# SSD mixer: channel tiles in pairs, one f32 run for a pair's mixed parts and the next pair's turns, states with 256 moving columns

## The chip, the cores and the metric

The kernel runs on one core of a Trainium2 chip. The metric is the device time of one execution in microseconds, median of several. A profile is one execution recorded by the hardware profiler. The engines are PE (matrix multiply, with PEld its weight loads), DVE (vector), ACT (activation functions, copies, casts), POOL (hardly used here) and SP (issues the DMAs). Each works through its own queue in order and waits at semaphores for the others.

## The reference

A trunk of two layers over 512 tokens and 1024 channels. Layer 0 mixes with Mamba-2 SSD, layer 1 with HGRN2; each has a squared-ReLU MLP, post-LayerNorm and a gated embedding. The change concerns the SSD mixer alone: 2048 inner channels (32 heads of 64), 4 groups, state size 128, chunks of 128 tokens.

```python
z, xbc, dt = jnp.split(u @ w_in, [SSD_D_INNER, SSD_D_INNER + SSD_CONV_DIM], axis=-1)
xbc = jax.nn.silu(causal_depthwise_conv(xbc, conv_w, conv_b))
xs, bm, cm = jnp.split(xbc, [SSD_D_INNER, SSD_D_INNER + SSD_BC_DIM], axis=-1)
...
cb = jnp.einsum('bclgn,bcsgn->bcgls', cm, bm)
y_diag = jnp.einsum('bcgls,bcgrls,bcsgrp->bclgrp', cb, decay, xdt)
decay_to_end = jnp.exp(a_cs[:, :, -1:] - a_cs)
states = jnp.einsum('bclgn,bclgr,bclgrp->bcgrpn', bm, decay_to_end, xdt)
...
y_off = jnp.einsum('bclgn,bcgrpn,bclgr->bclgrp', cm, prev, jnp.exp(a_cs))
y = y_diag + y_off + d_skip.astype(jnp.float32).reshape(g_, r_)[:, :, None] * xs
y = y.reshape(bsz, seq, SSD_D_INNER) * jax.nn.silu(z.astype(jnp.float32))
y = rms_norm(y.reshape(bsz, seq, g_, SSD_D_INNER // g_), norm_w.reshape(g_, SSD_D_INNER // g_))
return y.reshape(bsz, seq, SSD_D_INNER).astype(u.dtype) @ w_out
```

## The kernel before

The SSD inner channels form 16 tiles of 128 channels (two heads each), indexed j; four tiles are one group, with one B and one C projection per group. The loop `for j in range(17)` (L740 on) runs over them. For a tile:

- `x_part(j)` and `z_part(j)`: two projections. `project` splits weights into a high and a low f32r part (ACT casts `whi`, L110; DVE subtracts `wlo`, L112) and issues 24 f32r matmuls of 512 moving columns (L116 to L118). Weights are loaded from HBM by SP (L103) into 3 raw buffers and split into 6 pairs of buffers ahead of their use. x goes through a convolution of four taps (one step on ACT, L570, three on DVE, L573) and SiLU (L574) to `xs`; z through SiLU to `sz`.
- `turn_x(j)`: four PE transposes of xs (L635), read by DVE into `xw` (L639) and `xdt` (L641).
- `decays(j)`: from a table of cumulative decays (`csd`, loaded by DMA into `a`) DVE and ACT make `m` (L654, L659, L660), `ecs` (L658, L661) and `cd`.
- `states(j)`: three f32 matmuls of 128 moving columns (L669) and five short DVE operations that form `pv` (L675 to L678).
- `mixed(j)`: 14 f32 matmuls of half width, two beside each other in the array's column halves (L687, L689).
- `finish(j)`: DVE forms y (L705, L706), ACT and DVE its f32r parts `ys` (L708, L709), ACT squares it (L711) and DVE adds the square to `ss` of the group (L715).

`rms_group(g)` sums `ss` over channels by matmuls (L721) and makes `ri`; `pieces(g)` then gives the eight parts of the group's output projection (L250 adds them to `acc`), issued two at a time between the tiles. `bc_prep` makes `btok` and `cbm` for a group (L598, L604, L600, L606). The last group's output projection is `out_project`, with layer norm, transposes and their split (L230, L235, L236) chunk by chunk, behind which the MLP starts.

PE's order is that of the program text (`manual_schedule`); the orders of DVE, ACT and SP are set by a scheduler that goes by priorities, and are fixed when the program is built. PSUM has eight banks: four for projections (`psj`), and one each for `pt`, `pm`, `py0`, `py1`. In the loop a step for j runs: x projection, `states(j - 1)`, `mixed(j - 2)` and `finish`, z projection, `turn_x(j)`, `decays(j)`, two pieces. The f32 work of a tile so stands in two runs on PE: states with mixed, and the turn.

Of the kernel before, what the change touches and what calls it, by code (L numbers as in the profile page):

```python
# [15 lines left out]
P = 128  # L16
T = 512
NCH = 4
# [23 lines left out]
def trunk(ctx: ExitStack, tc, a):  # L42
# [27 lines left out]

    two = dict(cv=2, cm=2, cbm=2, pv=2)
    mlp = dict(r=8, blk=2, sg=2)
    bufs = dict(ssd=dict(two, xs=3, sz=3, btok=2, xdt=2, xw=2, ecs=2, ss=2), mlp0=mlp, hgrn=dict(qx=2, f=2, k=4, qo=2, qt=4, xc=2, gg=2, tot=4, sc=2, scd=2, btok=2), mlp1=mlp)
    phase = []
# [14 lines left out]
    def bank(p, tag):  # L89
        return mk(p, [P, T], tag)  # L90
# [445 lines left out]
    nc.vector.scalar_tensor_tensor(r1, up, -1.0, ab, ALU.add, ALU.subtract)  # L536
    ru = row("cbm")
    nc.vector.reciprocal(ru, up)
# [55 lines left out]

    def bc_prep(bcm, pt, spare):
# [5 lines left out]
        pc = bank(psy, spare)  # L601
# [10 lines left out]
    prep, live, decay = {}, {}, {}  # L612

# [6 lines left out]
    def z_part(j):  # L620
        ps = projected(10 * (j // 4) + 3 + 2 * (j % 4))
        sz = tmp("sz", [P, T])
        nc.scalar.activation(sz, ps, AF.Silu)
        live[j].append(sz)

# [4 lines left out]

    def turn_x(j, pt):
        dt_tok, w_tok, cs_tok = toks
        xs = live[j][0]
        for c in range(NCH):
            nc.tensor.transpose(pt[:, c * P : (c + 1) * P], xs[:, c * P : (c + 1) * P], ident)  # L635
        hs = slice(2 * j, 2 * j + 2)
        ptv = pt.rearrange("p (c h q) -> p c h q", c=NCH, h=2)
        xw = tmp("xw", [P, 3, 2, 64])
        nc.vector.tensor_mul(xw, ptv[:, 0:3], bc(w_tok[:, 0:3, hs], 3, 64))  # L639
        xdt = tmp("xdt", [P, NCH, 2, 64])  # L640
        nc.vector.tensor_mul(xdt, ptv, bc(dt_tok[:, :, hs], 3, 64))  # L641
        live[j] += [xw, xdt]

    def decays(j):
        dt_tok, w_tok, cs_tok = toks
        csb = decay.pop(j)
        btok, cbm, cm = prep[j // 4]
        cd = mk(sm, [P, 2, NCH], "cd")
        nc.scalar.activation(cd, csb.rearrange("p h (c l) -> p h c l", c=NCH)[:, :, :, P - 1], AF.Exp)
        m = mk(w4, [P, 2, T], "b")  # L650
# [10 lines left out]
        nc.vector.tensor_mul(ecs, ecs, bc(cm[:, P:], 1, 2))  # L661
        live[j] += [cd, m, ecs]

    def states(j):
        xs, sz, xw, xdt, cd, m, ecs = live[j]
        btok = prep[j // 4][0]
        pst_ = bank(psm, "pm")
        for c in range(3):
            nc.tensor.matmul(  # L669
                pst_[:, c * P : (c + 1) * P], btok[:, c, :], xw[:, c].rearrange("p h q -> p (h q)"), start=True, stop=True  # L670
            )
        pv = tmp("pv", [P, 3, 2, 64])
        stv = pst_[:, : 3 * P].rearrange("p (c h q) -> p c h q", c=3, h=2)
        with tc.high_priority(offset=LEAD + SOON):
            nc.vector.tensor_copy(pv[:, 0], stv[:, 0])  # L675
            for c in range(1, 3):
                nc.vector.tensor_mul(pv[:, c], pv[:, c - 1], bc(cd[:, :, c], 2, 64))
                nc.vector.tensor_add(pv[:, c], stv[:, c], pv[:, c])  # L678
        live[j].append(pv)

    def mixed(j):
        xs, sz, xw, xdt, cd, m, ecs, pv = live.pop(j)
        yd = bank(psy, "py%d" % (j % 2))
# [33 lines left out]
    def rms_group(g, pr):  # L717

        for c in range(NCH):
            for r in range(0, P, 64):  # L720
                nc.tensor.matmul(  # L721
                    pr[r : r + 64, 64 * c : 64 * c + 64], ss[g][:, c * P + r : c * P + r + 64], ones_s, start=True, stop=True
                )
# [13 lines left out]
    outs = iter(())  # L737
    bcm = {}
    with tc.manual_schedule(engines={mybir.EngineType.PE}):
        for j in range(17):  # L740
            if j < 16:
                load_decay(j)
                if j % 4 == 0:
                    bcm[j // 4] = bc_group(j // 4)
                x_part(j)
            if j == 0:
                z_part(0)
                continue
            if j == 4:
# [3 lines left out]
            if j == 1:  # L753
                z_part(1)
                prep[0] = bc_prep(bcm[0], bank(pst, "pt"), "py0")
                toks.extend(dt_tail())
                turn_x(0, bank(psy, "py1"))
                decays(0)
                continue
            if j == 2:  # L760
                turn_x(1, bank(pst, "pt"))
                decays(1)
                states(0)
                z_part(2)
                states(1)
                finish(0, *mixed(0))
                turn_x(2, bank(pst, "pt"))
                decays(2)
                continue
            if j == 16:  # L770
                next(outs), next(outs)
            states(j - 1)
            done = mixed(j - 2)
            if j % 4 == 2 and j > 2:
                outs = pieces(j // 4 - 1, rms_group(j // 4 - 1, bank(psy, "py1")))
            finish(j - 2, *done)
            if j < 16:
                z_part(j)
                if j % 4 == 0:
                    prep[j // 4] = bc_prep(bcm[j // 4], bank(psm, "pm"), "py1")  # L780
                turn_x(j, bank(pst, "pt"))
                decays(j)
                next(outs, None), next(outs, None)
        next(outs)
        finish(15, *mixed(15))
        next(outs)
        for _ in outs:
            pass
    h_s, *after = norm(0)
# [493 lines left out]
```

## Time and profile before

| | |
|---|---|
| median of 3 runs | 1422.53 us (1421.46 to 1422.73) |
| profiled execution | 1422.3 us, span 1420.5 us |
| granted clock of PE | 1.00 |
| SSD loop in the trace | from about 15 to 350 us |
| DVE in 350 to 390 us (output projection of the last group, norm) | 38.85 us busy |

In the profile a line number is that of the source line that issued an instruction; a helper's line (L110, L116) collects all its callers, so the names of the tiles tell which work it is. A row of a group gives busy time, mean duration of one in ns, and the idle time of the engine before it with what ended it. In a timeline each row gives start, length, engine, line, and in brackets the wait ahead. PE's matmuls are pipelined: a row's length is longer than the distance to the next, and the distance is what a matmul costs.

### The profile page before, as it was taken

The numbers are of one execution on the slowest core, as the hardware profiler recorded it, in microseconds if no ns is written. First come the engines' busy times: TensorE is split into PE (matmuls) and PEld (weight loads), VectorE is DVE, ScalarE is ACT, GpSimd is POOL, SyncE is SP. The second block draws the span as 40 slices with busy tenths as digits, with TensorE's granted clock in tenths as the row PEclk, the third lists the DMA queues.
The fourth block names the chain that finished last, engine by engine and source line by source line (L and its number), as shares of the span: only waits on it lengthen the run. The fifth ranks groups of instructions, "written<-read, shape, count | busy, mean of one in ns | idle before, by whom it ended". The sixth has DMA issues, their size and how long they took to land.

```text
span 1420.5 us, 20454 instructions
## 1 busy us (share of the span) xinstructions
PE 1413.6 (100%) x8143; PEld 1182.3 (83%) x8143; DVE 1025.4 (72%) x1713; ACT 744.4 (52%) x1089; POOL 1.6 (0%) x9
## 2 busy tenths in 40 slices
PE   9999999999999999999999999999999999999998
PEld 7888888888888888888888888888898888888887
DVE  7987777778967667677963774776785867667873
ACT  7776656664265454545543446465454544544641
POOL 0000000000000000000000000000000000000000
PEclk9999999999999999999999999999999999999999
DMA  8343333233433444442422222222163444444231
GB/s 292 127 145 108 113 118 101 95 104 124 158 119 127 156 133 149 134 148 104 149 90 91 92 92 72 90 90 76 60 238 104 148 147 135 149 133 163 89 119 45
DMA packets 48960, 174.83 MB, mean 123 GB/s; under 512 B 5728, under 2 KB 6368, under 8 KB 48736
## 3 DMA queue, kind: packets, MB, share of 16 engines
q1 hardware_dynamic: 48864, 173.52, 35.9%
q8 instruction: 64, 1.05, 0.3%
q14 instruction: 32, 0.26, 0.1%
HBM read 171.34 MB, written 2.16 MB: 122 GB/s over the span
## 4 chain that ended last, share of the span: by engine, by line
PE 96%; DVE 2%; DMA 1%; ACT 0%; issue 0%; SPq 0%
PE pj L116 25%; PE pj L118 25%; PE pj L117 25%; PE py L116 5%; PE py L118 5%; PE py L117 5%; PE py L687 1%; PE py L942 1%; PE pm L669 1%; PE py L689 1%; PE pt L635 0%; PE pt L230 0%; DMA acc<-in_xw 0%; PE pm L230 0%; DVE wlo L112 0%; DVE b L236 0%
## 5 line engine op out<-in xcount | busy, mean ns | idle before, releaser
L110 ACT CAST whi<-raw 128x1024 fp32r<-128x1024 f32 x226 | 237.1, 1050 | 377.8 <-PE pj L117 264.6
L112 DVE TENSOR_TENSOR wlo<-raw,whi 128x1024 fp32r<-128x1024 f32 x226 | 274.3, 1220 | 159.1 <-ACT whi L110 155.0
L116 PE MATMUL pj<-b,whi 128*128 128x512 f32 (+1 forms) x1008 | 381.5, 379 | 0.2 <-ACT b L235 0.2
L117 PE MATMUL pj<-b,whi 128*128 128x512 f32 (+1 forms) x1008 | 379.4, 376 | 0.7 <-DVE b L236 0.7
L118 PE MATMUL pj<-b,wlo 128*128 128x512 f32 (+1 forms) x1008 | 378.9, 376 | 0.0
L118 PE MATMUL pj<-whi,b 128*128 128x512 f32 (+1 forms) x592 | 229.5, 388 | 0.0
L116 PE MATMUL pj<-whi,b 128*128 128x512 f32 (+1 forms) x584 | 229.3, 393 | 0.0
L117 PE MATMUL pj<-wlo,b 128*128 128x512 f32 (+1 forms) x584 | 226.1, 387 | 0.0
L116 PEld LDWEIGHTS pj<-b,whi 128*128 128x128 f32 x1008 | 189.5, 188 | 36.2 <-issue 1.7
L118 PEld LDWEIGHTS pj<-b,wlo 128*128 128x128 f32 x1008 | 189.8, 188 | 34.7
L117 PEld LDWEIGHTS pj<-b,whi 128*128 128x128 f32 x1008 | 189.8, 188 | 34.6 <-DVE b L236 0.9
L118 PEld LDWEIGHTS pj<-whi,b 128*128 128x128 f32 x592 | 111.3, 188 | 22.9 <-DVE b L1137 0.2
L116 PEld LDWEIGHTS pj<-whi,b 128*128 128x128 f32 x584 | 109.8, 188 | 22.7 <-ACT k L871 0.5
L117 PEld LDWEIGHTS pj<-wlo,b 128*128 128x128 f32 x584 | 109.8, 188 | 21.2
L110 ACT CAST whi<-r 128x1024 fp32r<-128x1024 f32 x64 | 67.4, 1053 | 63.8 <-PE pj L118 35.6
L112 DVE TENSOR_TENSOR wlo<-r,whi 128x1024 fp32r<-128x1024 f32 x64 | 78.0, 1219 | 22.2 <-ACT whi L110 22.0
L118 PE MATMUL py<-whi,b 128*128 128x512 f32 x216 | 84.2, 390 | 0.0
L117 PE MATMUL py<-wlo,b 128*128 128x512 f32 x192 | 74.8, 389 | 0.0
L116 PE MATMUL py<-whi,b 128*128 128x512 f32 x192 | 74.4, 389 | 0.0
L573 DVE SCALAR_TENSOR_TENSOR cv<-pj,cst,cv 128x509 f32<-128x509 f32 (+2 forms) x66 | 49.0, 742 | 8.7 <-ACT cv L570 8.4
L118 PEld LDWEIGHTS py<-whi,b 128*128 128x128 f32 x216 | 40.5, 188 | 8.5
L116 PEld LDWEIGHTS py<-whi,b 128*128 128x128 f32 x192 | 36.1, 188 | 7.6
(321 smaller groups left out, 1816.0 us busy)
## 6 DMA issues: line engine op xcount, KB each, us to landing
raw<-in_w SPq DMA_DIRECT2D x112, 512.0 KB, 3.2
r<-in_w SPq DMA_DIRECT2D x64, 512.0 KB, 3.5
raw<-in_wssd SPq DMA_DIRECT2D x38, 512.0 KB, 3.7
a<-csd SPq DMA_DIRECT2D x16, 512.0 KB, 3.5
raw<-in_wso SPq DMA_DIRECT2D x16, 512.0 KB, 3.4
raw<-in_wg SPq DMA_DIRECT2D x16, 512.0 KB, 3.4
raw<-in_whvg SPq DMA_DIRECT2D x16, 512.0 KB, 3.3
raw<-in_whq SPq DMA_DIRECT2D x16, 512.0 KB, 3.4
```

The source lines that it names most:

```text
L110: nc.scalar.copy(hi[:, :n], f)
L112: nc.vector.tensor_sub(lo[:, :n], f, f32(hi[:, :n]))
L116: nc.tensor.matmul(out, sh, mh, start=start, stop=False, **kw)
L117: nc.tensor.matmul(out, sh, ml, start=False, stop=False, **kw)
L118: nc.tensor.matmul(out, sl, mh, start=False, stop=stop, **kw)
L573: nc.vector.scalar_tensor_tensor(cv[:, d:], ps[:, : T - d], convw[:, i, k : k + 1], cv[:, d:], ALU.mult, ALU.add)
L669: nc.tensor.matmul(pst_[:, c * P : (c + 1) * P], btok[:, c, :], xw[:, c].rearrange("p h q -> p (h q)"), start=True, stop=True)
L687: nc.tensor.matmul(yd[64 * r : 64 * r + 64, sl], xdt[:, c, r, :], m[:, r, sl], start=True, stop=c == 0)
L689: nc.tensor.matmul(yd[64 * r : 64 * r + 64, sl], pv[:, c - 1, r, :], ecs[:, r, (c - 1) * P : c * P], start=False, stop=True,)
L942: nc.tensor.matmul(ps[r][32 * b : 32 * b + 32, base + n * c : base + n * c + n], kk[r][:, ts], moving(r, 4 * c + b), start=True, stop=True,)
```

## The change

The loop goes by pairs, k = 1 to 8. `turn_x` becomes `turn_pair`: eight transposes into two banks, and one `xw` for both tiles. `states(k)` does a pair with three matmuls of 256 moving columns into the banks `pt` and `pm`, and DVE's operations on `pv` are twice as wide. The two `mixed` parts of pair k - 1 and the turns of pair k follow each other; ahead of the turns, for even k, stands `bc_prep` of a new group, which now uses two `psj` banks. z projections of a pair move into the step after its x projections, ahead of `mixed`. The rms matmuls use full width (four instead of eight) and a `psj` bank, and stand right behind `states` for k = 3, 5, 7. Four pieces go into each of the steps 3 to 6, eight into step 8 around the last two `mixed` parts. Buffers: four each of xs and sz, one of btok, cbm, xw, pv. What `some(n)` calls are the `pieces` of before.

```diff
-    def turn_x(j, pt):
+    def turn_pair(k, pts):
         dt_tok, w_tok, cs_tok = toks
-        xs = live[j][0]
-        for c in range(NCH):
-            nc.tensor.transpose(pt[:, c * P : (c + 1) * P], xs[:, c * P : (c + 1) * P], ident)
...
+        xw = tmp("xw", [P, 3, 2, 2, 64])
+        pair[k] = [xw, mk(sm, [P, 2, 2, NCH], "cd")]
+        for t, pt in enumerate(pts):
+            xs = live[2 * k + t][0]
+            for c in range(NCH):
+                nc.tensor.transpose(pt[:, c * P : (c + 1) * P], xs[:, c * P : (c + 1) * P], ident)
...
-    def states(j):
...
+    def states(k):
+        xw, cd = pair[k]
+        btok = prep[k // 2][0]
+        ps = bank(pst, "pt"), bank(psm, "pm")
+        st = [ps[c // 2][:, c % 2 * 256 : c % 2 * 256 + 256] for c in range(3)]
         for c in range(3):
-            nc.tensor.matmul(
-                pst_[:, c * P : (c + 1) * P], btok[:, c, :], xw[:, c].rearrange("p h q -> p (h q)"), start=True, stop=True
-            )
...
+            nc.tensor.matmul(st[c], btok[:, c, :], xw[:, c].rearrange("p t h q -> p (t h q)"), start=True, stop=True)
...
-            for r in range(0, P, 64):
-                nc.tensor.matmul(
-                    pr[r : r + 64, 64 * c : 64 * c + 64], ss[g][:, c * P + r : c * P + r + 64], ones_s, start=True, stop=True
-                )
+            nc.tensor.matmul(pr[:, 64 * c : 64 * c + 64], ss[g][:, c * P : (c + 1) * P], ones_s, start=True, stop=True)
...
+    PIECES = {3: (2, 2), 4: (2, 2), 5: (2, 2), 6: (2, 2)}
...
+        turn_pair(0, (bank(psy, "py1"), bank(psj, "pj")))
+        for k in range(1, 9):
+            i, j = 2 * k, 2 * k + 1
+            mine, theirs = PIECES.get(k, (0, 0))
+            decays(i - 2)
+            if k < 8:
+                if k in (4, 6):
+                    bcm[k // 2] = bc_group(k // 2)
+                x_part(i)
+            else:
+                finish(13, *held[:2], z_part(13))
+                z_part(14)
+            states(k - 1)
+            if k in (3, 5, 7):
+                outs = pieces(k // 2 - 1, rms_group(k // 2 - 1, bank(psj, "pj")))
+            decays(i - 1)
+            some(mine)
+            if k < 8:
+                load_decay(i)
+                x_part(j)
                 load_decay(j)
...
+            some(theirs)
+            if k == 1:
+                bcm[1] = bc_group(1)
+            elif k < 7:
+                z_part(i - 2)
+                z_part(i - 1)
...
+            done = [mixed(i - 2), (mixed(i - 1))] if k != 7 else [mixed(12)]
...
+            if k < 8:
+                if k % 2 == 0:
+                    prep[k // 2] = bc_prep(bcm[k // 2], bank(psj, "pj"), bank(psj, "pj"))
+                turn_pair(k, (bank(pst, "pt"), bank(psm, "pm")))
+            for t, d in enumerate(done):
+                finish(i - 2 + t, *d)
```

The instructions that move are seen in the engines' queues. PE before, around the first rms matmuls (tile 5's states, tile 4's mixed part; L721 are the rms matmuls of group 0, `ss_629` its sum of squares):

```order
L669 MATMUL pm_1183<-xw_1123,btok_978 128x128 x3
L687 MATMUL py_201_1193<-b_998,xdt_994 64x128 x4
L689 MATMUL py_201_1193<-ecs_1007,pv_1056 64x128 x2
L687 MATMUL py_201_1193<-b_998,xdt_994 64x128 x2
L689 MATMUL py_201_1193<-ecs_1007,pv_1056 64x128 x2
L687 MATMUL py_201_1193<-b_998,xdt_994 64x128 x2
L689 MATMUL py_201_1193<-ecs_1007,pv_1056 64x128 x2
L721 MATMUL py_202_1208<-ones_s_169,ss_629 64x64 x8
L116 MATMUL pj_1229<-b_5_111,whi_1232 128x512
```

PE now at the same rms matmuls (L729, in the step k = 3): the end of the projection `pj_1029` of tile 6, whose 24 matmuls follow the long run with the turns of tiles 4 and 5, then the states of pair 2, the rms and the first piece of the output projection.

```order
L117 MATMUL pj_1029<-b_8_114,whi_1032 128x512
L118 MATMUL pj_1029<-b_6_112,wlo_1034 128x512
L679 MATMUL pt_1067<-xw_981,btok_971 128x256 x2
L679 MATMUL pm_1068<-xw_981,btok_971 128x256
L729 MATMUL pj_1078<-ones_s_169,ss_734 128x64 x4
L116 MATMUL pj_1112<-whi_1102,b_115_727 128x512
```

Between the last mixed part of the group (tile 3) and these rms matmuls stood two projections, one turn, and other tiles' states and mixed part; now there are bc_prep's matmuls, the turns, one projection and the states. DVE before, where the last square is added to `ss_629` (L715): the turn's products follow, and the copy of the next states (L675) comes later.

```order
L705 SCALAR_TENSOR_TENSOR y_1077<-xs_689,cst_165,py_178_1062 128x512
L654 TENSOR_SCALAR b_1129<-a_1012,toks_462 128x128
L706 TENSOR_TENSOR y_1077<-y_1077,sz_760 128x512
L654 TENSOR_SCALAR b_1129<-a_1012,toks_462 128x128 x6
L709 SCALAR_TENSOR_TENSOR b_98_623<-y_1077,cst_165,b_97_622 128x512
L715 TENSOR_TENSOR ss_629<-ss_629,sq_1082 128x512
L639 TENSOR_TENSOR xw_1123<-pt_1118,toks_462 128x384
L641 TENSOR_TENSOR xdt_1125<-pt_1118,toks_462 128x512
```

DVE now at the same sum (L724, `ss_734`, with the square of tile 3, `sq_1010`): the copy of the next pair's states (L683) and two of its pv steps stand ahead of it.

```order
L714 SCALAR_TENSOR_TENSOR y_1005<-xs_594,cst_165,py_153_951 128x512
L669 TENSOR_TENSOR b_1015<-b_1015,cbm_977 128x1024
L715 TENSOR_TENSOR y_1005<-y_1005,sz_929 128x512
L683 COPY pv_1072<-pt_1067 128x256
L670 TENSOR_TENSOR ecs_1024<-ecs_1024,cm_672 128x768
L685 TENSOR_TENSOR pv_1072<-pv_1072,cd_982 128x256
L718 SCALAR_TENSOR_TENSOR b_116_728<-y_1005,cst_165,b_115_727 128x512
L686 TENSOR_TENSOR pv_1072<-pt_1067,pv_1072 128x256
L724 TENSOR_TENSOR ss_734<-ss_734,sq_1010 128x512
```

ACT before, at the square of tile 3 (L711):

```order
L658 ACTIVATE ecs_1138<-a_1012 128x768
L649 ACTIVATE cd_1271<-a_1143 128x8
L574 ACT_TABLE_LOAD
L574 ACTIVATE xs_1045<-cv_1046 128x512
L708 ACTIVATE b_97_622<-y_1077,cst_165 128x512
L711 ACTIVATE sq_1082<-y_1077 128x512
```

ACT now, at the same square (L720): a weight cast (L110) and the convolution's first step of tile 6 (L570) stand before the part of y that DVE's L718 needs (L717).

```order
L667 ACTIVATE ecs_1095<-a_863 128x768
L110 CAST whi_1246<-raw_1244 128x1024
L656 ACTIVATE cd_1309<-a_1140 128x8
L110 CAST whi_1360<-raw_1358 128x1024
L570 ACTIVATE cv_1061<-pj_1029,cst_165 128x512
L717 ACTIVATE b_115_727<-y_1005,cst_165 128x512
L720 ACTIVATE sq_1010<-y_1005 128x512
```

The group's last sum has moved, in DVE's queue, from ahead of the next states' copy to behind it, and its square, in ACT's, from behind tile 5's SiLU to behind tile 6's first convolution step.

More of the change, by code (lines that the diff above doesn't have):

```diff
@@ L69, in f32 @@
         return t.bitcast(F32)
-    two = dict(cv=2, cm=2, cbm=2, pv=2)
+    two = dict(cv=2, cm=2)
     mlp = dict(r=8, blk=2, sg=2)
-    bufs = dict(ssd=dict(two, xs=3, sz=3, btok=2, xdt=2, xw=2, ecs=2, ss=2), mlp0=mlp, hgrn=dict(qx=2, f=2, k=4, qo=2, qt=4, xc=2, gg=2, tot=4, sc=2, scd=2, btok=2), mlp1=mlp)
+    bufs = dict(ssd=dict(two, xs=4, sz=4, xdt=2, ecs=2, ss=2), mlp0=mlp, hgrn=dict(qx=2, f=2, k=4, qo=2, qt=4, xc=2, gg=2, tot=4, sc=2, scd=2, btok=2), mlp1=mlp)
     phase = []
@@ L536, in trunk @@
     nc.vector.scalar_tensor_tensor(r1, up, -1.0, ab, ALU.add, ALU.subtract)
-    ru = row("cbm")
+    ru = row("btok")
     nc.vector.reciprocal(ru, up)
@@ L593, in bc_group, with bc_prep @@
         return bcm
-    def bc_prep(bcm, pt, spare):
+    def bc_prep(bcm, pt, pc):
         bm, cm = bcm
@@ L600, in bc_prep @@
         nc.scalar.copy(btok, pt[:, : 3 * P].rearrange("p (c n) -> p c n", c=3))
-        pc = bank(psy, spare)
         for c in range(NCH):
@@ L611, in trunk @@
     toks = []
-    prep, live, decay = {}, {}, {}
+    prep, live, decay, pair = {}, {}, {}, {}
     def x_part(j):
@@ L623, in z_part @@
         nc.scalar.activation(sz, ps, AF.Silu)
-        live[j].append(sz)
+        if j in live:
+            live[j].insert(1, sz)
+        return sz
     def load_decay(j):
@@ L752, in trunk @@
                     nc.vector.tensor_scalar(acc[:, c, :], acc[:, c, :], ALPHA, None, ALU.mult)
[L753 to L788, printed above, removed]
+            done = [mixed(i - 2), (mixed(i - 1))] if k != 7 else [mixed(12)]
+            if k == 7:
+                live[13].insert(1, None)
+                held = mixed(13)
+            if k < 8:
[4 more added lines that the diff above has]
+                finish(i - 2 + t, *d)
+        some(4)
     h_s, *after = norm(0)
```

68 lines of the change are left out of this document (39 added, 29 removed).

## The prediction

> **What bounds the kernel now.** I read the page's first part and its chain that ended last, then the PE's waits, then single stretches of the timeline.
>
> ```profile
> PE 1413.6 (100%) x8143; PEld 1182.3 (83%) x8143; DVE 1025.4 (72%) x1713; ACT 744.4 (52%) x1089; POOL 1.6 (0%) x9
> PE 96%; DVE 2%; DMA 1%; ACT 0%; issue 0%; SPq 0%
> 40.00:350.00 310.00, 309.51 (x1822) 258.53 (x1821) 246.59 (x473) 200.14 (x241) 0.00 (x0) 1.00 0.33 111
> ```
>
> The third row is a view of windows: the SSD loop from 40 to 350 us (its columns: length, busy PE, PEld, DVE, ACT, POOL, granted clock, DMA share, GB/s). PE is busy for 309.5 of 310 us at clock 1.00 and carries 96% of the chain. So whatever PE no longer executes is gained, and **whatever it newly waits for is lost**, one for one. DVE is busy for 80% of the loop: it has slack on average, not at every place. The profiled execution took 1422.3 us (span 1420.5 and 1.8 around it); the median shown is 1422.53. The sum is made on 1422.3; the difference is nothing here.
>
> **What the change saves on PE.** Projections are f32r matmuls, one every 0.227 us. Between them stand runs of plain f32 matmuls, each recorded as two passes (a transpose as one). Timeline of PE: start, length, group, idle before.
>
> ```profile
> 63.23 0.83 PE L669 MATMUL pm<-xw,btok 128*128 128x128 f32 x6
> 66.24 0.40 PE L118 MATMUL pj<-b,wlo 128*128 128x512 f32 x1
> ...
> 145.91 0.60 PE L635 MATMUL pt<-cst,xs 128*128 128x128 f32 x4
> 146.81 0.40 PE L118 MATMUL pj<-whi,b 128*128 128x512 f32 x1
> ...
> 342.89 0.39 PE L118 MATMUL pj<-whi,b 128*128 128x512 f32 x1
> 343.21 0.66 PE L687 MATMUL py<-b,xdt 128*64 128x128 f32 x8
> 343.69 0.39 PE L689 MATMUL py<-ecs,pv 128*64 128x128 f32 x4
> 343.91 0.39 PE L687 MATMUL py<-b,xdt 128*64 128x128 f32 x4
> 344.89 0.50 PE L116 MATMUL pj<-whi,b 128*128 128x512 f32 x1
> ...
> 57.24 0.66 PE L635 MATMUL pt<-cst,xs 128*128 128x128 f32 x4
> 57.66 0.47 PE L116 MATMUL pj<-b,whi 128*128 128x512 f32 x1
> 58.20 0.40 PE L118 MATMUL pj<-b,wlo 128*128 128x512 f32 x1
> ```
>
> I measure a run from its first f32 matmul to the third f32r one after it, less two regular steps (0.454). States with mixed: 66.24 - 63.23 - 0.45 = 2.56. A turn alone: 146.81 - 145.91 - 0.45 = 0.45. A pair of tiles takes two of each: **6.0 us**.
> After the change a pair has one long run and one states run. Two 64-column matmuls run side by side, and such a pair of passes takes 0.11 (343.69 to 343.91: two in 0.22). A mixed part is 14 of them, 1.53; with the changes of tile width at both ends it is 1.68 (343.21 to 344.89), and 0.09 is lost ahead of it (342.89 to 343.21 is 0.32). Four transposes take 0.42, the exit 58.20 - 57.66 - 0.45 = 0.09. So the long run is 0.09 + 1.68 + 1.53 + 0.85 + 0.09 = 4.24.
> No f32 matmul of before has 256 moving columns. Bounds: 0.109 a pass, as with 128 (if the weight load sets the pace), and 0.218, twice that (if the columns do).
>
> ```profile
> L669 PEld LDWEIGHTS pm<-xw,btok 128*128 128x128 f32 x96 | 13.1, 191 | 1.2
> L635 PEld LDWEIGHTS pt<-cst,xs 128*128 128x128 f32 x60 | 7.0, 140 | 2.9 <-ACT xs L574 1.8 <-ACT cd L649 0.2
> L721 PEld LDWEIGHTS py<-ones_s,ss 128*64 128x64 f32 x48 | 1.8, 138 | 0.0
> 120.29 0.63 PE L721 MATMUL py<-ones_s,ss 128*64 128x64 f32 x16
> 120.85 0.50 PE L116 MATMUL pj<-b,whi 128*128 128x512 f32 x1
> ```
>
> The rms passes have 64 moving columns and go by in pairs: eight in under 0.56, less than 0.07 each, against 0.109 for 128 columns with equally wide weights. Time goes with the moving columns, 0.85 ns each. The transposes say the same at full width: their loads are far shorter than those of L669, their passes are no faster. So I take 0.214: six passes, 1.28, plus 0.03 at the ends, 1.31 for a pair's states. The new pair is 4.24 + 1.31 = 5.55, a gain of 0.45; another 0.05 is the slower steps after two runs that are gone. **Eight pairs: -4.0** (-3.0 to -5.0).
> [...]
>
> The rms matmuls now load 128 weight columns for 64 moving ones. A load of 128 takes 191 ns and of 64 takes 138 (rows above): 53 ns per 64 columns, so 0.107 a pass, eight passes 0.86 against some 0.47: four times +0.4, less a simpler exit at the last, **+1.3** (0 to +1.6).
> One stall of before should go, since xs now has two projections ahead of its turn: **-0.5** (0 to -0.7).
>
> ```profile
> 71.93 0.66 PE L635 MATMUL pt<-cst,xs 128*128 128x128 f32 x4 [0.49 <-ACT xs L574]
> ```
>
> At the start turn_pair(0) needs xs of tile 1 right after that of tile 0, 5 us earlier than before; ACT has it about 0.25 late: **+0.25** (0 to +0.5). DVE loses five of ten short pv operations a pair and gains wider ones, beside PE: nothing. DMAs are the same in number, only later or earlier: nothing, since weights are six units ahead; without that cover each would cost its landing of 3.2 to 3.7 us.
>
> **What it adds: a wait ahead of the rms matmuls.** Before, the last sum of squares was ready long ahead:
>
> ```profile
> 112.39 0.68 DVE L715 TENSOR_TENSOR ss<-ss,sq 128x512 f32<-128x512 f32 x1
> ```
>
> It ended at 113.07, the rms matmuls began at 120.29. Now finish() of two tiles comes in one burst after the long run, and the rms stands only one projection and a states run later (k = 3, 5, 7). DVE's steps, start to start, by its timeline; then ACT's groups:
>
> ```profile
> 59.70 0.75 DVE L709 SCALAR_TENSOR_TENSOR b<-y,cst,b 128x512 fp32r<-128x512 f32 x1
> 60.37 0.68 DVE L641 TENSOR_TENSOR xdt<-pt,toks 128x512 f32<-128x512 f32 x1
> 60.97 1.65 DVE L654 TENSOR_SCALAR b<-a,toks 128x128 f32<-128x128 f32 x8
> 62.53 0.96 DVE L661 TENSOR_TENSOR ecs<-ecs,cm 128x768 f32<-128x768 f32 x1
> 63.40 1.22 DVE L112 TENSOR_TENSOR wlo<-raw,whi 128x1024 fp32r<-128x1024 f32 x1
> 64.54 0.29 DVE L675 COPY pv<-pm 128x128 f32<-128x128 f32 x1
> 64.74 1.22 DVE L660 TENSOR_TENSOR b<-b,cbm 128x1024 f32<-128x1024 f32 x1
> 65.87 0.29 DVE L677 TENSOR_TENSOR pv<-pv,cd 128x128 f32<-128x128 f32 x1
> ...
> L110 ACT CAST whi<-raw 128x1024 fp32r<-128x1024 f32 x54 | 56.4, 1046 | 66.0 <-PE pj L117 50.4 <-PE pj L118 8.3 <-DMA raw<-in_wssd 7.2
> L570 ACT ACTIVATE cv<-pj,cst 128x512 f32<-128x512 f32 x22 | 16.9, 769 | 0.0
> L708 ACT ACTIVATE b<-y,cst 128x512 fp32r<-128x512 f32 x16 | 11.4, 712 | 9.0 <-DVE y L706 9.0
> L711 ACT ACTIVATE sq<-y 128x512 f32<-128x512 f32 x12 | 7.4, 616 | 0.0
> ```
>
> Steps: 0.67 (L709, and L705 like it), 0.60 (512 columns), 0.20 (128), hence some 0.34 for 256, 0.87 (768), 1.13 (1024), 1.56 for eight L654. Let S be the start of the states run. Ahead of it lie 10.8 us: two mixed parts (3.3), bc_prep's passes and the turns (2.1), a projection (24 x 0.227). The first mixed part ends 1.8 into that, at S - 9.0, and finish() of its tile can begin on DVE. From there, at k = 5 and 7, DVE has in order: y, 8 L654, y*sz, cbm, two xw (0.5 each), two xdt, ys.lo, ss, the second y, m*cbm, y*sz, ecs: 0.67 + 1.56 + 0.6 + 0.6 + 1.0 + 1.2 + 0.67 + 0.6 + 0.67 + 1.13 + 0.6 + 0.87 = 10.2, to S + 1.2. Then comes the copy of the states to pv (which waits for PE until S + 1.1), to S + 1.5. The next, ys.lo, needs ys of ACT, and ACT has ahead of it a weight cast whose buffer PE frees at about S: 0.95 + 0.72 and a handover, S + 1.7. Then 0.67, a pv product 0.34, the sum 0.68 and 0.05 handover: **S + 3.45**. PE is through with the states at S + 1.31: it waits 2.15.
> At k = 3 the same count reaches the copy in time (S + 1.0), but DVE's order has another 0.87 (ecs) and another pv step (0.34) between copy and sum: 1.1 + 0.34 + 0.87 + 0.34 + 0.67 + 0.34 + 0.68 + 0.05 = S + 4.4, a wait of 3.1. Together **+7.4** (6.3 if 256 columns cost DVE no more than 128; 8.9 if each dependent step costs its full length). Behind the waiting rms stand all PE's later matmuls; nobody else hurries for it.
>
> **The end of the stage.**
>
> ```profile
> 372.25 0.28 PE L116 MATMUL pj<-b,whi 128*128 128x256 f32 x1
> 376.57 0.60 PE L230 MATMUL pt<-cst,acc 128*128 128x128 f32 x4
> 378.32 0.68 DVE L236 TENSOR_TENSOR b<-pt,b 128x512 fp32r<-128x512 f32 x1
> 386.58 0.68 DVE L236 TENSOR_TENSOR b<-pt,b 128x512 fp32r<-128x512 f32 x1
> 387.31 0.39 PE L117 MATMUL pj<-b,whi 128*128 128x256 f32 x1 [0.67 <-DVE b L236]
> ```
>
> PE waits here for the last chunk's L236, which follows the third chunk's by 8.26 us of DVE rows of the same kind before and after. The third chunk's transposes came 4.3 us after the output projection's end (372.25); in the new order they stand behind two half projections instead of one and a half, at 5.8, so that L236 moves by at least 1.1: **+1.5** (0 to +2.5).
>
> **Sum**: -4.0 - 0.5 + 1.3 + 0.25 + 7.4 + 1.5 = +5.95, 1428.2 us.
>
> **Rivals.** (a) *The sums are in time*: the mechanism at one place, L729 at k = 3, 5, 7, which costs 7.4 only if DVE's last sum ends after S + 1.26. If DVE came through its rows 3 us sooner there, PE would not wait: 1420.8, and 1418 with the end unchanged. For: 7.2 us of slack before; DVE idles 20%. Against: its rows start only when mixed ends, and they are in order. Chance 0.15.
> (b) *The weight load sets the pace of full-width passes*: then 256 columns go by in 0.109, 48 passes x 0.105 = -5.0. PE reaches the rms 0.65 sooner and waits 0.65 longer, three times: 1425.1. For: a load of 128 columns takes those 0.107. Against: the tile pairs and the transposes above. Chance 0.10.
> (c) *More waits*: four projection banks are freed only 0.3 to 0.5 us ahead of their reuse by the same reckoning (conv after a weight cast, k = 3 to 6), and tile 15's turn has as little; a lag of 1 us on DVE makes each a stall: +3 to +5, 1432. A clock that drops in the new gaps belongs here:
>
> ```profile
> L150 PE MATMUL pm<-y 128*128 128x128 f32 x16 | 3.7, 428 | 1.0 <-DVE y L147 1.0
> ```
>
> the first passes, after idleness, take 3.7 us for 16, twice the later pace; such a stretch after a gap loses 1.8. [...] No run here shows it: the clock is 1.00 in every row, with no gap over 1. Chance of (c) 0.13.
>
> **How the numbers follow.** The forecast has 0.62: 1428.2, by its terms 1424 to 1431. The range 1419.5 to 1432 takes in (a), (b) and the lower half of (c). A difference below 0.2% (2.8 us) can't be told from none. Slower (above 1425.4): the forecast's most, (c), a part of (b), 0.70. Faster (below 1419.7): the better half of (a), 0.07. Within: 0.23.
>
> **What would show it.** Right: PE waits for DVE's ss at the rms matmuls three times, 2 to 3 us, the first the longest; long runs of some 4.2 us; states passes 0.214 apart. Wrong: no such wait; states passes at 0.11; or waits at other places above 1 us in sum.

## The result, and the profile after

The changed kernel takes **1433.17 us** (median of 6 runs, 1431.04 to 1434.46), the kernel before 1422.57 (6 runs): ratio 1.0074, 95% interval 1.0061 to 1.0087. It is slower, as forecast, but by 10.6 us where 5.7 were forecast, and 1.2 us above the range. The profiled execution took 1434.5 us, span 1432.4, mean granted clock 0.998; before it was 1422.3, 1420.5 and 1.00. The six executions differ by the clock: 1431.04 us at a mean of 1.000, 1432.05 and 1432.34 at 0.999, 1434.0 to 1434.46 at 0.998 and 0.996.

Where in the program the time is lost shows in the transposes of the normalizations (L230): those of the last chunk of the SSD stage, then the first ones behind the first MLP, the HGRN mixer and the second MLP. Timeline of PE, before and then after (start, length, engine, line; the windows are narrow, so that a row counts only the first matmuls):

```profile
384.63 0.38 PE L230 MATMUL pt<-cst,acc 128*128 128x128 f32 x2
703.28 0.38 PE L230 MATMUL pt<-cst,acc 128*128 128x128 f32 x2
1018.74 0.29 PE L230 MATMUL pt<-cst,acc 128*128 128x128 f32 x1
1357.80 0.27 PE L230 MATMUL pt<-cst,acc 128*128 128x128 f32 x1
```

```profile
394.02 0.41 PE L230 MATMUL pt<-cst,acc 128*128 128x128 f32 x2 [0.89 <-DVE acc L221]
714.05 0.27 PE L230 MATMUL pt<-cst,acc 128*128 128x128 f32 x1
1029.38 0.38 PE L230 MATMUL pt<-cst,acc 128*128 128x128 f32 x2
1369.74 0.27 PE L230 MATMUL pt<-cst,acc 128*128 128x128 f32 x1
```

The lag is 9.4 us at the end of the SSD stage, the only one that the change edits. But it is 10.8 behind the first MLP, 10.6 behind the HGRN mixer, and 11.9 behind the second MLP: each MLP, whose code is untouched, costs 1.3 more. So there are two things to explain.

**Inside the stage**, the waits of PE over the whole changed kernel (total, times, longest):

```profile
PE pj L729 <- DVE ss L724: 6.9, 3, 3.0
...
PE pt L230 <- DVE acc L221: 0.9, 1, 0.9
PE pj L117 <- DVE b L236: 0.7, 1, 0.7
PE pj L639 <- ACT xs L574: 0.6, 1, 0.6
```

The rms matmuls wait for the group's last sum of squares three times, as forecast. The wait at k = 3 in the timeline of both engines:

```profile
106.69 0.59 PE L679 MATMUL pm<-xw,btok 128*128 128x256 f32 x2
106.91 0.42 DVE L683 COPY pv<-pt 128x256 f32<-128x256 f32 x1
...
109.44 0.68 DVE L724 TENSOR_TENSOR ss<-ss,sq 128x512 f32<-128x512 f32 x1
110.27 1.08 PE L729 MATMUL pj<-ones_s,ss 128*128 128x64 f32 x8 [2.98 <-DVE ss L724]
```

The sum stands behind the copy of the next states in DVE's queue and ends at 110.12; DVE is not idle from 105 to 115 us (first rows of the windows below). PE could have begun at 107.13 (the last of two passes, 0.215 apart, at 106.91, and 0.22). The gap is 3.1 us, and 2.1 at k = 5 and at k = 7: 7.4 us together (the view of waits counts from the end that is modelled for the last pass, hence its 6.9).

Windows of 5 us around the three waits (busy time of PE, PEld, DVE, ACT, POOL, then the granted clock, DMA share, GB/s):

```profile
105.00:110.00 5.00, 2.29 (x11) 1.63 (x9) 5.00 (x9) 4.14 (x5) 0.00 (x0) 1.00 0.00 0
110.00:115.00 5.00, 4.73 (x18) 3.91 (x19) 5.00 (x16) 2.20 (x4) 0.00 (x0) 0.68 0.00 0
115.00:120.00 5.00, 5.00 (x23) 4.16 (x22) 3.56 (x5) 2.54 (x3) 0.00 (x0) 0.98 0.68 206
...
200.00:205.00 5.00, 3.04 (x17) 2.50 (x16) 5.00 (x11) 4.14 (x5) 0.00 (x0) 0.90 0.00 0
205.00:210.00 5.00, 5.00 (x19) 4.04 (x19) 4.66 (x14) 3.73 (x5) 0.00 (x0) 0.76 0.16 55
...
295.00:300.00 5.00, 3.23 (x18) 2.84 (x19) 5.00 (x13) 2.96 (x5) 0.00 (x0) 1.00 0.00 0
300.00:305.00 5.00, 5.00 (x24) 4.14 (x23) 4.22 (x10) 4.78 (x6) 0.00 (x0) 1.00 0.40 137
```

Behind the first two waits the granted clock falls, by 5 x (0.32 + 0.02) = 1.7 us and 5 x (0.10 + 0.24) = 1.7 us of clock in this execution. By the starts of the matmuls (427 ns apart for some 3.4 us, instead of 227) PE loses 1.5 and 1.6 us against the same stretch behind the third wait, where the clock stays at 1.00: 3.1 us. PE is busy meanwhile, so no wait shows it.

**In the MLPs**, PE waits for nothing more than before. Its matmuls are slower where they read one kind of tile, blk, as the moving operand. Rows of blk's own view, before and then after (x count: duration in ns, minimum, median, maximum; first and last start; form):

```profile
L117 PE MATMUL pj<-wlo,blk x64: 388/389/393, 464.0 to 1327.4; 128*128 128x512 f32 x64
...
L117 PE MATMUL py<-wlo,blk x64: 388/389/390, 496.6 to 1357.3; 128*128 128x512 f32 x64
```

```profile
L117 PE MATMUL pj<-wlo,blk x64: 393/394/398, 473.5 to 1339.2; 128*128 128x512 f32 x64
...
L117 PE MATMUL py<-wlo,blk x64: 393/396/398, 506.3 to 1369.3; 128*128 128x512 f32 x64
```

The six groups of 64 matmuls on blk have medians 5 to 8 ns higher, and the starts are 231 and 236 ns apart in turn instead of 227. Counted from the starts, that is 1.26 us in the first MLP and 1.27 in the second, against 0.03 and 0.00 before. What the change did to blk is in the allocation: `cd` grew from 32 to 64 bytes a partition in a pool with two buffers, and every tile allocated behind it starts 64 bytes further, blk at byte 173568 instead of 173504.

So the 11.9 us between the two profiled executions are 7.4 (waits) + 3.1 (clock) + 2.5 (blk) and -1.1 for everything else, where the forecast had +7.4 and -1.45.

### The profile page after: what moved, and what is told of

It reads as the page before. It is cut to its first block, busy times and chain, and to the rows that moved or that the text cites. A ratio compares the mean times of both kernels' runs of the same rounds, so it can differ in the third digit from the quotient of the medians.

```text
span 1432.4 us, 20277 instructions
## 1 busy us (share of the span) xinstructions
PE 1417.2 (99%) x8063; PEld 1183.9 (83%) x8063; DVE 1023.5 (71%) x1673; ACT 738.7 (52%) x1085; POOL 1.6 (0%) x9
## 4 chain that ended last, share of the span: by engine, by line
PE 92%; DVE 5%; ACT 1%; DMA 1%; issue 0%; SPq 0%; ACTq 0%
PE pj L116 24%; PE pj L117 24%; PE pj L118 24%; PE py L116 5%; PE py L117 5%; PE py L118 5%; PE py L960 1%; PE py L696 1%; DMA acc<-in_x 1%; DVE wlo L112 1%; PE py L698 0%; PE pt L230 0%; DMA acc<-in_xw 0%; PE pm L230 0%; ACT whi L110 0%
## 5 line engine op out<-in xcount | busy, mean ns | idle before, releaser
L110 ACT CAST whi<-raw 128x1024 fp32r<-128x1024 f32 x226 | 237.1, 1051 | 404.0 <-PE pj L117 277.6
L116 PE MATMUL pj<-b,whi 128*128 128x512 f32 (+1 forms) x1008 | 380.5, 378 | 0.2 <-ACT b L235 0.2
L116 PE MATMUL pj<-whi,b 128*128 128x512 f32 (+1 forms) x584 | 229.8, 394 | 0.1
L116 PEld LDWEIGHTS pj<-b,whi 128*128 128x128 f32 x1008 | 189.5, 188 | 34.7 <-ACT b L235 0.5
L116 PEld LDWEIGHTS pj<-whi,b 128*128 128x128 f32 x584 | 110.5, 189 | 23.3 <-ACT k L889 0.5
L110 ACT CAST whi<-r 128x1024 fp32r<-128x1024 f32 x64 | 67.1, 1049 | 65.0 <-PE pj L118 36.8
L116 PE MATMUL py<-whi,b 128*128 128x512 f32 x192 | 74.4, 389 | 0.0
L573 DVE SCALAR_TENSOR_TENSOR cv<-pj,cst,cv 128x509 f32<-128x509 f32 (+2 forms) x66 | 48.9, 743 | 2.8 <-ACT cv L570 2.4
L116 PEld LDWEIGHTS py<-whi,b 128*128 128x128 f32 x192 | 36.0, 188 | 7.6
```

Source lines behind the costliest of these rows:

```text
L110: nc.scalar.copy(hi[:, :n], f)
L116: nc.tensor.matmul(out, sh, mh, start=start, stop=False, **kw)
L573: nc.vector.scalar_tensor_tensor(cv[:, d:], ps[:, : T - d], convw[:, i, k : k + 1], cv[:, d:], ALU.mult, ALU.add)
```

## The experiments

Each kernel was measured beside runs of the kernel before on the same chip (medians 1422.2 to 1422.6 us). Ratios are to those runs.

### Two causes that the forecast's sum did not have: addresses and the clock

**b_pad32**: the kernel before, with all tiles of the stages shifted by 64 bytes.

```diff
-    nc.gpsimd.memset(mk(pad, [P, 16], "pad"), 0.0)
+    nc.gpsimd.memset(mk(pad, [P, 32], "pad"), 0.0)
```

> The kernel before with one number changed: the tile pad is 128 instead of 64 bytes a partition, so that every tile of the stages' own pools starts 64 bytes further, as in the changed kernel (the first blk tile of both MLPs at byte 173568 instead of 173504); the work is the same. Theory A (the start address of the moving operand sets the step of the f32r matmuls that read blk): the steps of 227 ns become 231 and 236 in turn in the MLPs' blk products, about +1.3 us in each of the two MLPs, 1425.1 us in all (1422.5 + 2.6). Rival B (the slow steps of the changed kernel come from a clock that has not come back whole after its pauses, or from other traffic at that time): 1422.5, steps of 227 ns as before.

Measured: 1425.21 us, ratio 1.0020 (1.0011 to 1.0029). Its row of blk, of the same view as above:

```profile
L117 PE MATMUL pj<-wlo,blk x64: 393/394/399, 464.2 to 1330.1; 128*128 128x512 f32 x64
```

The change's own slow row, without the change: 1.28 us lost in each MLP by the starts. Theory A holds, and B falls, since the clock of this run is 1.00.

**a_pad32** (the same edit in the changed kernel) and **a_pad64** (`[P, 64]` there).

> The changed kernel with the tile pad at 128 bytes a partition: the stages' tiles start another 64 bytes further, blk at 173632, which leaves the remainder 64 by 128 as before the change. Theory A: the blk products are back at 227 ns a step, the time falls by 2.6 us from the changed kernel's 1433.2 to 1430.6. Rival B: 1433.2. If only the exact old addresses are quick (a remainder of 192 by 256), it stays at 1433.2 too, while the kernel before with the same pad is slower.

> The changed kernel with the tile pad at 256 bytes a partition: blk starts at byte 173760, whose remainder by 256 is 192, that of the weight tiles (17088, 41664) and of the b8 tiles (66240), as in the kernel before (173504). The starts 173568 and 173632 (remainders 0 and 64) both gave slow steps. Theory A2 (the remainder by 256 decides, within the whole or against the other operands): blk products at 227 ns a step, 2.6 us less than the changed kernel, 1430.6 us at the same clock. Rival (only the old address, or another thing that the shift moves): steps of 231 and 236 ns as before, 1433.2.

Measured: a_pad32 1435.15 us (1.0081, 1.0067 to 1.0095), a_pad64 1430.76 us (1.0057, 1.0044 to 1.0070). Their rows of blk, in this order:

```profile
L117 PE MATMUL pj<-wlo,blk x64: 390/394/405, 474.6 to 1340.9; 128*128 128x512 f32 x64
```

```profile
L117 PE MATMUL pj<-wlo,blk x64: 389/389/393, 472.3 to 1335.5; 128*128 128x512 f32 x64
```

A start at 173632 is slow still, 1.19 us in each MLP, though its remainder by 128 is that of 173504, so the forecast of a_pad32 missed; at 173760, 256 bytes from the old start, the old pace is back (389 ns). (a_pad32's median is 2 us above the changed kernel's because its clock lost more: 0.996 in the profiled run.)

**b_all64**: the kernel before with weights, projection inputs and the stages' tiles all shifted by 64 bytes.

```diff
     nc.gpsimd.memset(ones_s, 1.0 / 512)
+    nc.gpsimd.memset(mk(cpool, [P, 16], "spare"), 0.0)
```

> The kernel before with a spare tile of 64 bytes a partition among the constants: weights (whi at 17152, wlo at 41728), the b8 tiles (66304), and the stages' tiles (blk at 173568) all move by 64 bytes together, to the remainder 0 by 256. Theory A3 (what counts is where the moving operand lies against the weights, since both are read at once): nothing slows, 1422.3 us, blk at 227 ns. Theory A4 (the remainder of the moving operand alone counts): nearly all of the some 5300 full-width f32r matmuls go at 231 to 236 ns, 6.7 ns more each, +35 us: 1457.

Measured: 1422.30 us, ratio 0.9998 (0.9989 to 1.0007), and blk, at the very byte 173568 that is slow in two other kernels, is quick:

```profile
L117 PE MATMUL pj<-wlo,blk x64: 389/389/397, 464.7 to 1327.9; 128*128 128x512 f32 x64
```

So theory A3 is the one that fits these runs: blk was quick where it had moved against the weights by 0 bytes (before, b_all64) or 256 (a_pad64), with medians of 389 ns, and slow where by 64 (after, b_pad32) or 128 (a_pad32), with 393 to 398. Whether it is the weights, or tiles that other engines read at the time, no run shows.

**a_fill**: busywork for PE in the three waits.

```diff
     def rms_group(g, pr):
 
+        for _ in range((13, 9, 9, 0)[g]):
+            nc.tensor.matmul(pr[:, :P], ident, ident, start=True, stop=True)
```

> The changed kernel with idle work in the waits: 13 transposes of the identity ahead of the rms matmuls of the first group, 9 ahead of those of the second and third, written to the bank that the rms matmuls overwrite (26 and 18 passes of 0.109 us: 2.8 and 2.0 us of waits of 3.1 and 2.1). The waits' length stays, but PE is busy in them. Theory C (the pause itself lowers the clock): no stretch at 0.50 behind the rms matmuls, clock 1.000, time 1431.0 (the changed kernel's quickest run) with less spread than 1431.0 to 1434.5. Rival D (the clock falls for another reason, such as the row of float32 matmuls or the power of that stretch): 1433.2 and windows at 0.50 as before.

Measured: 1430.03 us (1429.64 to 1431.13), ratio 1.0055 (1.0043 to 1.0068), 3.1 us below the changed kernel's median. Timeline of PE at k = 3 and the window behind it:

```profile
105.48 3.06 PE L729 MATMUL pj<-cst 128*128 128x128 f32 x26
108.62 1.08 PE L731 MATMUL pj<-ones_s,ss 128*128 128x64 f32 x8
```

```profile
108.00:113.00 5.00, 4.92 (x28) 4.18 (x28) 5.00 (x16) 2.17 (x4) 0.00 (x0) 1.00 0.00 0
```

The rms matmuls begin as late as before, 3.1 us behind the states, but the clock stays at 1.00 in every window of the stage. So the pause itself lowered the clock: in the changed kernel gaps of 3.1 and of 2.1 us were enough, and behind them the clock is 0.50 in windows of 1 us (112 to 115, 204 to 207) and the matmuls start every 427 ns.

The third gap of the changed kernel is as long as the second and leaves the clock alone. The traces have a pattern for this. In the changed kernel's trace the clock changes at 5.99, 111.81, 115.22, 203.97 and 207.38 us, and the distances are 31, 1, 26 and 1 times 3.413 us. Windows on that grid, at k = 5 and at k = 7:

```profile
200.55:203.96 3.41, 1.45 (x9) 1.00 (x8) 3.41 (x8) 3.39 (x5) 0.00 (x0) 1.00 0.00 0
203.97:207.37 3.40, 3.40 (x12) 2.92 (x12) 3.40 (x11) 1.38 (x3) 0.00 (x0) 0.50 0.00 0
...
292.71:296.12 3.41, 2.10 (x10) 1.47 (x8) 3.41 (x7) 2.80 (x4) 0.00 (x0) 1.00 0.00 0
296.12:299.53 3.41, 2.76 (x16) 2.46 (x17) 3.41 (x7) 1.61 (x3) 0.00 (x0) 1.00 0.00 0
```

The gap at k = 5 lies whole in one step of the grid, and the clock is low in the next step; the gap at k = 7 is cut in two (1.5 and 0.6 us by the starts of the matmuls). It is the same in a_pad32, a_pad64 and a_rms64, where the gap at k = 7 is cut into 1.5 and 0.6, 1.7 and 0.4, 1.9 and 0.2. A limit for one step does not account for all of it: the 1.9 us in a_rms64 did not lower the clock, while at k = 3 in a_pad64 1.6 us in each of two steps did. No run moved a gap against the grid, so this is a reading of the traces and not shown.

### The waits

**a_late**: the rms matmuls and the pieces behind them put behind x_part of the pair's second tile.

```diff
             states(k - 1)
-            if k in (3, 5, 7):
-                outs = pieces(k // 2 - 1, rms_group(k // 2 - 1, bank(psj, "pj")))
             decays(i - 1)
-            some(mine)
+            if k not in (3, 5, 7):
+                some(mine)
...
                 load_decay(j)
+            if k in (3, 5, 7):
+                outs = pieces(k // 2 - 1, rms_group(k // 2 - 1, bank(psj, "pj")))
+                some(mine)
             some(theirs)
```

> The changed kernel with rms_group and the two pieces behind it moved from behind states(k-1) to behind x_part(j), 24 projection matmuls of 0.227 us (5.4 us) later. Theory: PE no longer waits at the rms matmuls (3.1 + 2.1 + 2.1 = 7.4 us go) and the granted clock no longer falls to 0.50 behind them (up to 3.1 us): 1423 to 1426 us with a clock of 1.000, no wait for the ss add. Rival: the wait only moves, to the banks or to the pieces that need the reciprocal: 1428 or more.

Measured: 1430.28 us, ratio 1.0054 (1.0042 to 1.0067). The time is the rival's: the waits for the sum are gone, but others stand in their place. PE's waits, and the window at the second:

```profile
PE pm L639 <- ACT xs L574: 2.7, 1, 2.7
PE pj L116 <- ACT ri L731: 2.2, 2, 1.1
```

```profile
305.00:310.00 5.00, 3.67 (x11) 3.09 (x12) 4.62 (x17) 4.96 (x7) 0.00 (x0) 0.66 0.02 3
```

A projection needs the bank in which ACT still has to read the rms result; and tile 15's turn, which the third rms wait had covered, has to wait for xs, with a pause of 2.7 us behind which the clock falls again (0.66 in the window above).

**a_late2**: both mended, by another bank for the rms result and one piece that comes later (the edit is shown against a_late).

```diff
-    PIECES = {3: (2, 2), 4: (2, 2), 5: (2, 2), 6: (2, 2)}
+    PIECES = {3: (2, 2), 4: (2, 2), 5: (2, 2), 6: (2, 1)}
...
             if k in (3, 5, 7):
-                outs = pieces(k // 2 - 1, rms_group(k // 2 - 1, bank(psj, "pj")))
+                some(k == 7)
+                outs = pieces(k // 2 - 1, rms_group(k // 2 - 1, bank(pst, "pt")))
                 some(mine)
```

> As a_late (rms matmuls behind x_part of the pair's second tile), with the rms result in the bank pt instead of a pj bank, and one piece of the second group moved from k=6 to behind x_part(15) at k=7. In a_late three waits stood in the place of the ones removed: 1.1 us twice for the reciprocal's input to be read out of the pj bank (projection waits for L731), and 2.7 us for the xs of tile 15 at the turn of the last pair, with 1.7 us of low clock behind it. Theory: all of them go, 1430.3 - 2.2 - 2.7 - 1.7 = 1423.7 us, clock 1.000. Rival: DVE has no slack in these stretches, so that a wait of 1 us or more comes up elsewhere: 1426 or more.

Measured: **1423.57 us**, ratio 1.0006 (0.9997 to 1.0015), clock 1.000. One wait of 0.7 us for a bank is new:

```profile
PE pj L116 <- DVE cv L573: 0.7, 1, 0.7
```

9.6 us of the 10.6 that the change lost go with the later place of the rms matmuls and their pieces, with the bank and the piece moved to match. Blk is still slow in this kernel; c1 below is the same without that.

### The terms of the sum

**a_rms64**: the changed kernel with the rms matmuls in their old form, of 64 columns (the diff's lines in rms_group undone).

> The changed kernel with the rms matmuls in the old form, eight of 64 columns a group instead of four of 128. Theory (my term): from the first rms matmul to the projection behind it 0.4 us less in each of the four groups (0.81 to 0.41 in the last), some 1.3 us in all. Rival: the time is set by entry and exit of the row of float32 matmuls, less than 0.1 us a group. The waits for the ss add stay.

A single run: 1434.82 us, with a clock of 0.996. Timeline of PE at the third group, the changed kernel first, then a_rms64:

```profile
296.77 1.10 PE L729 MATMUL pj<-ones_s,ss 128*128 128x64 f32 x8 [1.96 <-DVE ss L724]
297.68 0.47 PE L116 MATMUL pj<-b,whi 128*128 128x512 f32 x1
```

```profile
297.08 0.69 PE L730 MATMUL pj<-ones_s,ss 128*64 128x64 f32 x16 [1.96 <-DVE ss L724]
297.70 0.50 PE L116 MATMUL pj<-b,whi 128*128 128x512 f32 x1
```

Behind a wait the wide form costs 0.91 us to the next projection, the narrow one 0.62: 0.3. In the last group, with no wait ahead, it is 0.81 against 0.62, but the projection ahead of the narrow form takes 0.31 instead of 0.23, and the net is 0.1. The width costs 3 x 0.3 + 0.1 = 1.0 us in four groups, not 1.3 to 1.6; the first two groups are taken to be like the third, since the low clock lies over them.

**s128**: a_late2 with the states in six matmuls of 128 columns.

```diff
         for c in range(3):
-            nc.tensor.matmul(st[c], btok[:, c, :], xw[:, c].rearrange("p t h q -> p (t h q)"), start=True, stop=True)
+            for t in range(2):
+                nc.tensor.matmul(
+                    st[c][:, t * P : t * P + P], btok[:, c, :], xw[:, c, t].rearrange("p h q -> p (h q)"), start=True, stop=True
+                )
```

> a_late2 with the states in six matmuls of 128 moving columns instead of three of 256. Theory (a float32 pass takes 0.109 us per 128 columns, whatever its width): the states run takes 12 x 0.109 instead of 6 x 0.215 us, 0.1 us more or less a pair, 1423.6 us within its spread. Rival (a pass costs its weight load too): 6 x 0.08 us a pair and more, 1427.

A single run: 1423.43 us (a_late2: 1423.57). The states run of one pair with the first projection matmuls behind it, in the timeline of PE, a_late2 and then s128:

```profile
75.83 1.02 PE L679 MATMUL pt<-xw,btok 128*128 128x256 f32 x4
76.70 0.59 PE L679 MATMUL pm<-xw,btok 128*128 128x256 f32 x2
76.94 0.58 PE L116 MATMUL pj<-b,whi 128*128 128x512 f32 x1
77.36 0.40 PE L117 MATMUL pj<-b,whi 128*128 128x512 f32 x1
```

```profile
76.65 1.05 PE L680 MATMUL pt<-xw,btok 128*128 128x128 f32 x8
77.54 0.61 PE L680 MATMUL pm<-xw,btok 128*128 128x128 f32 x4
77.90 0.48 PE L116 MATMUL pj<-b,whi 128*128 128x512 f32 x1
78.22 0.39 PE L117 MATMUL pj<-b,whi 128*128 128x512 f32 x1
```

From the first states matmul to the second projection matmul it is 1.53 us and 1.57, as the theory has it; no time of a weight load shows. The 256 moving columns of the change's title are worth 0.04 us a pair, which the time of one run can't show; what the change saves comes from fewer rows of float32 matmuls.

### Versions that join what was learnt

**c1** is a_late2 with the tile pad of 256 bytes. **c4** puts the rms matmuls into the long run, and the pieces one step later:

```diff
-    PIECES = {3: (2, 2), 4: (2, 2), 5: (2, 2), 6: (2, 2)}
+    PIECES = {4: (2, 2), 5: (2, 2), 6: (2, 2), 7: (2, 2)}
...
-            if k in (3, 5, 7):
-                outs = pieces(k // 2 - 1, rms_group(k // 2 - 1, bank(psj, "pj")))
...
                 turn_pair(k, (bank(pst, "pt"), bank(psm, "pm")))
+            if k in (3, 5, 7):
+                outs = pieces(k // 2 - 1, rms_group(k // 2 - 1, bank(psj, "pj")))
```

with the narrow rms form and the pad of 256 bytes. **c5** is c4 with `some(2)` for `some(4)` ahead of the last mixed parts and `some(6)` behind them.

> a_late2 (no waits at the rms matmuls, 1423.6 us) with the tile pad at 256 bytes, so that blk has the weights' remainder again (2.5 us in the traces of a_pad64 against the changed kernel). Theory: the two causes add, 1421.0 us. Rival: they overlap, 1423.

> The changed kernel with the tile pad at 256 bytes, the rms matmuls in the old form of 64 columns, and the rms matmuls of the first three groups put into the long row of float32 matmuls (behind turn_pair of k = 3, 5, 7), their pieces from k = 4, 6, 8 on. Theory: no wait for the ss add, and three rows of float32 matmuls fewer than a_late2, with 0.45 us for each rms instead of 0.92: 1421.0 - 3 x 0.47 - 0.08 = 1419.5 us. Rival: k = 3 has now too little projection between x_part(7) and the turn of the pair, and PE waits there for xs or for a bank: 1421 or more.

> c4 with two instead of four pieces of the third group ahead of the last pair's mixed matmuls and six instead of four behind them. Theory (the 0.9 us for which the transposes of the end wait for the residual sum on DVE come from finish(14) and finish(15) queued there just before): the wait goes, c4 less 0.9, 1418.6 us. Rival: mixed(14) then waits for its operands, c4 or slower.

| kernel | us | ratio to before (95%) |
|---|---|---|
| c1 | 1420.37 | 0.9985 (0.9977 to 0.9994) |
| c4 | 1419.51 | 0.9978 (0.9969 to 0.9987) |
| c5 | 1419.69 | 0.9980 (0.9971 to 0.9988) |

The causes add: c1 is 3.2 us below a_late2, where 2.6 were expected. c4 came out where it was expected, 3.1 us below the kernel before, but not all by the working: an rms behind a turn makes the long run 0.79 us longer (4.84 instead of 4.06, from its first matmul to the next f32r one), not 0.45. What made up for most of it is c1's wait of 0.7 us for a bank (L116 for L573, as in a_late2), which c4 doesn't have. c5's theory fell; the wait at the end of the stage is there as in c4:

```profile
PE pt L230 <- DVE acc L221: 0.9, 1, 0.9
```

What it rests on stands below, with the prediction's term for the end of the stage.

## Why the prediction was wrong

**Right**: the direction, and the mechanism that carried it. The term of 7.4 for the new wait at L729 came out as 7.4, with the longest gap (3.1 forecast, 3.1 measured) at k = 3 and 2.15 forecast, 2.1 measured at k = 5 and 7. The sum of squares does stand behind the states' copy, and DVE goes through its rows as worked out: the sum ends 3.4 us behind the start of the states run at k = 5 (3.45 forecast) and 4.3 at k = 3 (4.4).

**Right, with small errors of size**: the states' passes of 256 columns go by every 0.215 us (0.214 forecast), so that rival (b) falls. By the forecast's own way of counting, a states run takes 1.31 us and the long run of mixed parts and turns 4.24, both as forecast. The wider rms cost 1.0 where 1.3 stood, but behind its waits it now makes a row of its own besides: the rows of float32 matmuls as a whole, the rms's among them, came out 2.5 us cheaper by the starts of the matmuls, where -4.0 + 1.3 = -2.7 stood. The wait for xs in the old order is gone, but one of 0.6 us at the first pair stands in its place: +0.15 together by the starts, where -0.5 + 0.25 stood.

At the end of the stage 1.25 us were lost by the starts of the matmuls where 1.5 stood. DVE's last row ahead of the last chunk's transposes before, then the third chunk's transposes and DVE's rows behind them after:

```profile
383.12 1.27 DVE L221 SCALAR_TENSOR_TENSOR acc<-acc,lnrs,b 128x1024 f32<-128x1024 f32 x1
```

```profile
386.35 0.60 PE L230 MATMUL pt<-cst,acc 128*128 128x128 f32 x4
387.80 0.69 DVE L236 TENSOR_TENSOR b<-pt,b 128x512 fp32r<-128x512 f32 x1
392.60 1.28 DVE L221 SCALAR_TENSOR_TENSOR acc<-acc,lnrs,b 128x1024 f32<-128x1024 f32 x1
```

The third chunk's transposes stand 5.7 us behind the end of the output projection (380.61), where 5.8 was forecast and 4.3 stood before. From that chunk's first L236 to the end of the last chunk's L221 DVE takes 6.1 us without idle in both kernels (378.32 to 384.39, 387.80 to 393.88). So the forecast's chain holds, but PE is stopped by it one place earlier than named: for 0.9 us at L230, which needs L221, while L236 holds PE for 0.7 as before.

All terms but L729 make -1.1 together, forecast -1.45. Taken without the two causes below, the sum was right: a_fill, which has the late rms but no pause, took 1430.0, and less the 2.5 us of blk that is 1427.5, against 1428.2.

**The step that failed** is the sum's last line: it priced the gaps of 3.1, 2.15 and 2.15 us at their own length, and put the clock behind them at nothing. The lower clock behind them stood apart, as part of rival (c), "a clock that drops in the new gaps", with a chance of 0.13, though the forecast's own waits were those gaps. Its size was there: 1.8 us for one such stretch, against 1.5 and 1.6 measured. Two stretches belonged in the sum: 1431.8 at the forecast's price, 1431.3 as measured. The doubt (no gap over 1 us in the trace of before, the clock 1.00 in every row) was a reason for a wide range, not for leaving it out.

**What was nowhere in the prediction** is the 2.5 us of the MLPs. The working followed the change through the stage that it edits and took what comes behind as untouched. b_pad32 shows that 64 bytes of allocation cost the kernel before 3.0 us (1.6 to 4.1 by its interval) with no other edit. It took both causes to leave the range: the execution whose mean clock is 1.000 took 1431.04 us, and a_pad64, with a quick blk, 1430.76.

Rival (a) fell, since the sums were late as forecast. The other part of rival (c), stalls for banks and tile 15's turn, did not show in the changed kernel: a_late shows that the third rms wait had covered the one at tile 15's turn (2.7 us).

**Open**: what decides whether a gap of 2.1 us lowers the clock (the pattern of k = 5 and k = 7 is read, not tested), and whether blk's place counts against the weights or against another tile.

## What to carry to other kernels

A new wait on PE, where it is otherwise always busy, costs its length and can cost a lower clock behind it: the three here cost 7.4 us, and the clock behind two of them 1.5 and 1.6. Price both in the same line, and look for an order in which the consumer comes one projection later, which here gave back 9.6 of 10.6 us once the waits that it uncovered were mended. A tile that grew by 32 bytes, in two buffers, moved all tiles allocated behind it by 64, which cost 2.5 us in MLPs that nobody had edited, so compare the start addresses of matmul operands in untouched stages before you call them untouched. What was saved by joining rows of small matmuls, tenths of a microsecond a row and 2.5 us in all, one dependency that came due early took back, with its 7.4.

## What the runs showed of the hardware

- **Start addresses.** The f32r matmuls of 512 columns that read blk start every 227 ns in the trace of before, with blk at byte 173504, and every 233 on average (231 and 236 in turn) in the changed kernel's, with blk at 173568: 1.3 us for each MLP's 192 matmuls. Medians of their durations are 389 ns before, 394 to 397 in the changed kernel, 394 to 398 in b_pad32 (64 bytes off as well), 393 to 395 in a_pad32 (128 off), and 389 in a_pad64 (256 off). With weights, projection inputs and blk shifted all together by 64 bytes, they are 389 (b_all64, 1422.30 us). Whether the weights are what counts was not shown.
- **The clock.** In the changed kernel the granted clock was 0.50 for 3.4 us behind pauses of PE of 3.1 and of 2.1 us, and 1.00 behind another of 2.1; behind the first pause of a_pad32 and of a_rms64 it was 0.50 for 6.8 us. With the same delay filled by matmuls (a_fill) it was 1.00 in every window of the stage.
- **Columns.** Float32 passes of 256 columns start every 0.215 us in the changed kernel, and eight of 128 columns took 0.89 in s128, 0.11 each; the states run of a pair with its exit took 1.53 us in a_late2, with 256 columns, and 1.57 in s128, with 128.
